# Seven block products for eight in the down projection of a decoder layer

## The chip, the cores and the metric

The kernel runs on one core of a Trainium2 chip. The metric is the time of the kernel on the device in microseconds (us), the median of several runs. A profile of one execution is read beside the times.

## The reference

One decoder layer on 256 tokens of width 2048: a token mixer, a cross-attention and a gated feed-forward block, each with a norm before and after. Only the last block matters here:

```python
def conv_glu_ffn(h, w_up, conv_w, conv_b, w_down):
    u = h @ w_up
    uc = conv_b + sum(conv_w[j] * shift_right(u, CONV_WIDTH - 1 - j) for j in range(CONV_WIDTH))
    gate, up = split_cols(uc, (D_FF, D_FF))
    return (jax.nn.gelu(gate, approximate=True) * up) @ w_down
...
x = x + rms_norm(conv_glu_ffn(h, ffn_w_up[l], ...), ffn_post_norm[l])
```

The down projection is the product with `w_down`: 256 x 8192 by 8192 x 2048, in float32.

## The kernel before

**Float32 by parts.** TensorE multiplies in a reduced float32 type (`F32R`). Each operand is split into a high part (a cast to that type, on ScalarE) and a low part (the operand less the cast, on VectorE). A product is then three matmuls: high by high, low by high, high by low (`tm_products`, L467). The weights' parts are `wh` (`Feed.hi`, L431) and `wl` (`Feed.lo`, L457). The down projection's activations are kept as `ac`, 64 tiles of 128 features by 256 tokens (`actile`, L1701), and are split into `as` just before use (`asplit`, L1788), two tiles to a buffer, with two buffers (`au0`, `au1`). `split` (L239) makes one ScalarE cast and one VectorE subtraction for each tile.

**The order of the work.** All engines run in the order in which the program issues their instructions. `run` (L475) goes through a list of blocks. A block is one group of output columns; for each chunk of weights it asks the feed for the staged weights of the chunk up to three ahead (`feed.lo(i + 3)`, L511), for transfers up to seven ahead (`feed.dma(i + 7)`, L512; four `raw` buffers, filled through the queue of SP), takes the activations (`b["xs"](k)`, L510) and issues the products (L545). Between products `side.half()` lets a piece of other work, such as the evacuation of the block before, into the ScalarE and VectorE queues.

**The down projection** is the last two blocks (L1915), one for each half (1024) of the output columns. A chunk is one k tile of 128 features: 128 x 1024 weights, 512 KB. Both halves go through all 64 k tiles. For each k tile there are four PSUM banks, two token tiles by two column groups of 512, and three matmuls of 128x128 by 128x512 into each: twelve to a tile. The first half's four banks come from the pool `aux`, the second's from `acc`; together the pools have the eight banks of PSUM. The last four tiles of the second half are done bank by bank (`tail`, L556), so that its evacuation (`fd_evac`, L1842) can follow each bank. `asplit` for the next pair of tiles is called at each even tile (`ax`, L1800), so ScalarE's cast waits until TensorE has left the buffer of two pairs before.

The stage before it is the up projection (`fm` blocks). It ends with the evacuation of its last block (`fw_evac`, L1747), which makes the last `ac` tile. Its inputs `fx` lie in the buffer `hT`, which the end of the kernel uses again: `load_gain` (L1833), called at tile 24 of the first half, takes it over for the gain of the last norm and for half of the output.

Of the kernel before, what the change touches and what calls it, by code (L numbers as in the profile page):

```python
# [9 lines left out]
F32 = mybir.dt.float32  # L10
# [5 lines left out]
P = 128  # L16
D = 2048
S = 256
# [136 lines left out]
def _layer(ctx, tc, nc, d, dbg):  # L155
# [22 lines left out]
    def C(name, tag, shape=None, dt=F32):  # L178
        return mp.tile(shape or [P, S], dt, tag=tag, bufs=1, name=name)
# [10 lines left out]
    def mm(out, lhsT, rhs, start=True, stop=True):  # L190
        pe.matmul(out, lhsT, rhs, start=start, stop=stop, skip_group_check=True)  # L191
# [47 lines left out]
    def split(hi, lo, src):  # L239
        act.copy(hi, src)  # L240
        dve.tensor_sub(lo, src, hi)
# [138 lines left out]
    blocks = []  # L380

    def block(kind, srcs, xs, evac, before=None, cols=512, pool_=None, pre=None, bankwise=False, tail=0,
              two=False, wide=None):


        blocks.append(dict(kind=kind, srcs=srcs, xs=xs, evac=evac, before=before, cols=cols,
                           pool=pool_ or acc, pre=pre, task=None, bankwise=bankwise, tail=tail, two=two, wide=wide is not None, xw=wide))
        return blocks[-1]

    class Feed:  # L390
        def __init__(self):
            a, g = blocks[0]["srcs"], blocks[1]["srcs"]
            self.src = a[:LEAD] + [c for p in zip(a[LEAD:], g) for c in p] + g[len(a) - LEAD:]
            self.src += [s for b in blocks[2:] for s in b["srcs"]]
            self.raw, self.st, self.nd, self.ns, self.nl, self.nop = {}, {}, 0, 0, 0, 0

        def dma(self, upto):
# [33 lines left out]
        def hi(self, upto):  # L431
            while self.ns <= min(upto, len(self.src) - 1):
                self.dma(self.ns)
                r = self.raw[self.ns]
                wh = self.staged("wh", r)
                for o, v in self.pieces(self.ns, wh, r):
                    nc.scalar.copy(o, v)  # L437
                self.st[self.ns] = [wh, None]
                self.ns += 1

        def first(self, c):

# [14 lines left out]
        def lo(self, upto):  # L457
            self.hi(upto)
            while self.nl <= min(upto, len(self.src) - 1):
                r = self.raw.pop(self.nl)  # L460
                wl = self.staged("wl", r)
                for o, v, h in self.pieces(self.nl, wl, r, self.st[self.nl][0]):
                    nc.vector.tensor_sub(o, v, h)  # L463
                self.st[self.nl][1] = wl
                self.nl += 1

    def tm_products(o, t, c, wx, first, last):  # L467
        wh, wl, xh, xl = wx
        t = slice(t // P * P, t // P * P + P)
        wh, wl = (turns(w[:, c:c + 512]) for w in (wh, wl))  # L470
        mm(o, xh[:, t], wh, start=first, stop=False)
        mm(o, xl[:, t], wh, start=False, stop=False)
        mm(o, xh[:, t], wl, start=False, stop=last)

    def run():  # L475
        feed = Feed()
# [6 lines left out]
        def work(b):  # L483
# [14 lines left out]
            nt = len(b["srcs"]) if b["bankwise"] else b["tail"]  # L498
            if nt:
                b["srcs"], tail = b["srcs"][:-nt], b["srcs"][-nt:]  # L500
            for ci, s in enumerate(b["srcs"]):
                second = b["two"] and ci % 2
                if second:
                    k -= s.shape[1]
                if b["pre"]:
                    b["pre"](ci, feed)
                feed.lo(i + 1)
                side.half(True)
                side.more = lambda: feed.hi(i + 2)
                ahead = b["xs"](k)  # L510
                feed.lo(i + 3)  # L511
                feed.dma(i + 7)  # L512
                wh, wl = feed.st.pop(i)
                later = []
                for kj in range(s.shape[1]):
                    xh, xl = b["xs"](k) if kj else ahead
                    first, last = k == 0, k == nk - 1
                    if b["wide"]:
                        xw = b["xw"](k).rearrange("p h (a b) -> p h b a", a=2)
                        for m in range(nm):  # L520
                            a, c = (w[:, kj, m * P:(m + 1) * P] for w in (wh, wl))
                            mm(banks[m].rearrange("p h s -> p (h s)"), a, xw, start=first, stop=False)
                            mm(banks[m][:, 0], c, turns(xh), start=False, stop=last)
                    elif b["kind"] == "fm":
                        xh, xl = turns(xh), turns(xl)
                        for m in range(nm):
                            r = min(P, b["cols"] - m * P)
                            o = banks[second * 2 + m // 2][0:r, m % 2]
                            a, c = (w[:, kj, m * P:m * P + r] for w in (wh, wl))
                            mm(o, a, xh, start=(first and m % 2 == 0), stop=False)  # L530
                            if not (b["two"] and ci == 0):
                                mm(o, a, xl, start=False, stop=False)
                            mm(o, c, xh, start=False, stop=last)
                        if b["two"] and ci == 0:
                            later.append((kj, xl))
                        for j, v in later if len(later) == s.shape[1] else ():
                            for m in range(nm):
                                mm(banks[m // 2][:, m % 2], wh[:, j, m * P:(m + 1) * P], v, start=False, stop=False)
                    elif b["cols"] < 512:
# [67 lines left out]
    def W(name, blk):  # L607
        return [d[name][blk, c] for c in range(d[name].shape[1])]
# [1177 lines left out]
    M["as"] = {}  # L1786

    def asplit(k):  # L1788

        if k not in M["as"]:  # L1790
            n = k // 2
            a = mp.tile([P, 1024], F32R, tag=f"au{n % 2}", bufs=1, name="as")
            a = a.rearrange("p (i j s) -> p i j s", i=2, j=2)
            a, b_ = a[:, 0], a[:, 1]
            for j in range(2):
                split(a[:, j], b_[:, j], actile((k + j) % 64))
                M["as"][k + j] = (a[:, j], b_[:, j])
        return M["as"][k]

    def ax(n):  # L1800
        def xs(k):
            kk = n * 64 + k
            if kk == 58:
                side.need(fu["task"])
            if kk == 24:
                load_gain()
            if k % 2 == 0:
                asplit(kk)
                if kk + 2 < 128 and (k < 62 or n == 0):
                    asplit(kk + 2)  # L1810
            return M["as"].pop(kk)
        return xs

    def x_tokens():

        M["xt"] = []
        for f in range(4):
# [9 lines left out]
            for b in range(4):  # L1827
                for c in range(4):
                    act.copy(o[b * 32:b * 32 + 32, :, :, c], q[c * 32:c * 32 + 32, :, :, b].rearrange("p k t i -> p t k i"))
                    if c % 2:  # L1830
                        yield

    def load_gain():  # L1833
        end = mp.tile([P, 2, 2, 1024], F32, tag="hT", bufs=1, name="end")
        M["gain"], M["z3", 1] = end[:, 0].rearrange("p t c -> p (t c)"), end[:, 1]
# [6 lines left out]
    def fd_evac(n):  # L1842
# [69 lines left out]
            yield  # L1912
        return gen

    for n in range(2):  # L1915
        block("tm", W("w_fd", n), ax(n), fd_evac(n), cols=1024, pool_=acc if n else aux,
              tail=4 if n else 0)
    run()
    drain_bulk()

# [100 lines left out]
```

## Time and profile before

| | before |
|---|---|
| median of 3 runs | 1804.07 us (1803.82 to 1804.76) |
| span of the profiled execution | 1802.7 us |
| its own time | only the span is given |
| TensorE (PE) busy | 1793.1 us |
| VectorE (DVE) busy | 1325.1 us |
| ScalarE (ACT) busy | 1056.8 us |
| down projection: 1463.46 us to the end of its matmuls | 331.54 us, 1536 matmuls |
| mean granted TensorE clock | 0.999 |

Times in the profile are in us from the span's start. A matmul's busy time is longer than its share of the stream, as matmuls overlap: in an unbroken stretch the length divided by the count is what one costs. In the rows, `tm` and `fm` are PSUM banks, `wh`, `wl`, `as`, `raw` the tiles named above, and `tm<-wh,as` is the product of the two into the bank. L191 is the helper that issues every matmul, L68 the one that issues most ScalarE and VectorE operations, so tiles tell more than lines. `x128 | 48.6, 422` reads: 128 instructions, 48.6 us in all, 422 ns each; behind the second bar stands the engine's idle time ahead of them and who ended it. A timeline's row gives the start, the length of a merged run of instructions, and in brackets the idle time before it.

### The profile page before, as it was taken

How to read it: one execution, taken by the hardware profiler on the slowest of the kernel's cores; microseconds unless marked ns; L12 is line 12 of the kernel's file. 1: busy time of each engine (PE TensorE's matmuls, PEld its weight loads, DVE VectorE, ACT ScalarE, POOL GpSimd, SP SyncE). 2: the span in 40 equal slices, each digit the busy share in tenths (PEclk: the TensorE clock that was granted, in tenths of full speed). 3: DMA queues.
4: the chain of work that ended last, by engine and by line, in shares of the span. 5: the costliest groups of instructions: out<-in, count | busy, mean ns of one | idle time of the engine just before them, and what ended most of it. 6: DMA issues, size and time to landing. Idle time of an engine off the chain costs nothing.

```text
span 1802.7 us, 30168 instructions
## 1 busy us (share of the span) xinstructions
PE 1793.1 (99%) x11814; PEld 1636.5 (91%) x11814; DVE 1325.1 (74%) x1948; ACT 1056.8 (59%) x1642; POOL 28.7 (2%) x51
## 2 busy tenths in 40 slices
PE   9999999999999999999999999999999999999998
PEld 8999988888888999899999999999999988888887
DVE  7869995765765768789877788777777775666665
ACT  7576454654554665676666666665565564455454
POOL 0100000100100000000000000000000000000000
PEclk9999999999999999999999999999999999999999
DMA  8656564354556775556666666666666666666664
GB/s 282 206 170 187 164 188 151 120 177 154 188 190 207 246 233 176 187 170 189 210 199 201 208 195 204 209 194 201 207 195 200 205 203 218 208 204 207 201 200 151
DMA packets 99135, 351.61 MB, mean 195 GB/s; under 512 B 10896, under 2 KB 13968, under 8 KB 98864
## 3 DMA queue, kind: packets, MB, share of 16 engines
q1 hardware_dynamic: 97888, 347.38, 60.4%
q8 instruction: 93, 1.52, 0.3%
q0 software_dynamic: 384, 1.18, 0.3%
q10 hardware_dynamic: 720, 1.12, 0.2%
q14 instruction: 50, 0.41, 0.1%
HBM read 347.01 MB, written 2.10 MB: 194 GB/s over the span
## 4 chain that ended last, share of the span: by engine, by line
PE 99%; DVE 0%; DMA 0%; ACT 0%; issue 0%; SPq 0%; DVEq 0%; ACTq 0%
PE fm L191 55%; PE tm L191 39%; PE gram L191 0%; PE Y L191 0%; PE lv L191 0%; DMA op<-in_op_dram 0%; PE X L191 0%; PE num L191 0%; PE zwa L191 0%; PE U L191 0%; PE gramA L191 0%; PE xo L191 0%; PE zg L191 0%; PE Tn L191 0%; PE mT L1353 0%; PE st L191 0%
## 5 line engine op out<-in xcount | busy, mean ns | idle before, releaser
L463 DVE TENSOR_TENSOR wl<-raw,wh 128x1024 fp32r<-128x1024 f32 (+1 forms) x641 | 767.9, 1219 | 145.8 <-ACT wh L437 143.4
L437 ACT CAST wh<-raw 128x1024 fp32r<-128x1024 f32 (+1 forms) x641 | 656.0, 1044 | 109.7 <-PE tm L191 60.7
L191 PE MATMUL fm<-fx,wh 128*128 128x512 f32 (+1 forms) x2240 | 672.8, 364 | 0.6 <-DVE fx L68 0.4
L191 PE MATMUL fm<-fx,wl 128*128 128x256 f32 x2048 | 558.3, 273 | 0.0
L191 PEld LDWEIGHTS fm<-fx,wh 128*128 128x128 f32 x2240 | 409.2, 190 | 49.8 <-DVE fx L68 1.0
L191 PEld LDWEIGHTS fm<-fx,wl 128*128 128x128 f32 x2048 | 393.2, 192 | 0.0
L191 PE MATMUL tm<-wh,as 128*128 128x512 f32 x1024 | 304.6, 379 | 0.0
L191 PE MATMUL tm<-wh,hx 128*128 128x512 f32 (+1 forms) x832 | 243.9, 378 | 1.8 <-ACT hx L68 1.5
L191 PEld LDWEIGHTS tm<-wh,as 128*128 128x128 f32 x1024 | 193.5, 189 | 27.4
L191 PE MATMUL tm<-wl,as 128*128 128x512 f32 x512 | 194.0, 379 | 0.0
L68 ACT COPY ul<-fm 128x256 f32<-128x256 f32 x128 | 44.9, 373 | 225.1 <-PE fm L191 225.1
L191 PE MATMUL fm<-hx,wh 128*128 128x256 f32 x1024 | 174.5, 277 | 0.0
L191 PEld LDWEIGHTS tm<-wh,hx 128*128 128x128 f32 x832 | 151.0, 189 | 22.5 <-POOL wh L450 1.7
L191 PEld LDWEIGHTS fm<-hx,wh 128*128 128x128 f32 x1024 | 155.4, 192 | 1.1
L191 PE MATMUL tm<-wl,hx 128*128 128x512 f32 (+1 forms) x416 | 152.5, 373 | 0.1
L68 DVE TENSOR_TENSOR us<-fm,ul 128x256 f32<-128x256 f32 x128 | 48.5, 421 | 130.9 <-ACT ul L68 130.9
L191 PE MATMUL fm<-hx,wl 128*128 128x256 f32 x512 | 140.8, 275 | 0.0
L68 ACT CAST as<-ac 128x256 fp32r<-128x256 f32 x128 | 45.6, 405 | 153.0 <-PE tm L191 153.0
L68 DVE TENSOR_TENSOR as<-ac,as 128x256 fp32r<-128x256 f32 x128 | 48.6, 422 | 91.3 <-ACT as L68 91.3
L191 PEld LDWEIGHTS tm<-wl,as 128*128 128x128 f32 x512 | 96.8, 189 | 13.7
L191 PEld LDWEIGHTS fm<-hx,wl 128*128 128x128 f32 x512 | 98.3, 192 | 0.0
L191 PEld LDWEIGHTS tm<-wl,hx 128*128 128x128 f32 x416 | 77.5, 189 | 10.7 <-DVE wl L463 0.3
(374 smaller groups left out, 1883.8 us busy)
## 6 DMA issues: line engine op xcount, KB each, us to landing
raw<-in_w_fw_dram SPq DMA_DIRECT2D x232, 512.0 KB, 4.2
raw<-in_w_in_dram SPq DMA_DIRECT2D x160, 512.0 KB, 3.7
raw<-in_w_fd_dram SPq DMA_DIRECT2D x128, 512.0 KB, 4.0
raw<-in_w_br_dram SPq DMA_DIRECT2D x32, 512.0 KB, 4.3
raw<-in_w_mw_dram SPq DMA_DIRECT2D x24, 512.0 KB, 4.6
raw<-in_w_fu_dram SPq DMA_DIRECT2D x24, 512.0 KB, 4.0
raw<-in_w_mo_dram SPq DMA_DIRECT2D x8, 512.0 KB, 4.2
raw<-in_w_xk_dram SPq DMA_DIRECT2D x8, 512.0 KB, 4.3
```

Source lines behind the costliest of these rows:

```text
L68: return f(out, *a, **k)
L191: pe.matmul(out, lhsT, rhs, start=start, stop=stop, skip_group_check=True)
L437: nc.scalar.copy(o, v)
L463: nc.vector.tensor_sub(o, v, h)
```

## The change

Two neighbouring k tiles with two token tiles and two column groups make a product of two 2 x 2 block matrices: eight block products of three matmuls each. For seven pairs of tiles of each half (tiles 6 and 7, 14 and 15, to 54 and 55) the change computes the same sums with seven block products (the Strassen-Winograd form). In one of the fourteen pairs:

- VectorE makes four sums of blocks of weights (`sums`): three when the first tile of the pair is staged, one of them in place of the raw block, and one when the second is. The first three need both tiles' raw weights. Two low parts of the sums are added to `lo`, two ScalarE casts (1024 and 512 wide) to `hi`.
- VectorE makes four sums of blocks of activations in three instructions and splits them (one cast, one subtraction, 512 wide), in `asplit`.
- TensorE does 7 x 3 matmuls. Three of the products go straight into three of the old banks; the other four into four more banks (`more`), taken from the other pool, which collect over the seven pairs.

After the last pair the extra banks are combined and added into the four old banks by VectorE (`join_sums`). The first steps are issued at tile 56, the four additions into the banks at tile 57, each right behind that tile's products into the bank. The buffer `hT` is taken over at the first sum (`room`), and the split of `ac` is done for two tiles by one cast and one subtraction of 512, in all 64 pairs of tiles.

```diff
@@ class Feed
         def hi(self, upto):
             while self.ns <= min(upto, len(self.src) - 1):
                 self.dma(self.ns)
+                if self.ns in self.pairs:
+                    self.sums(self.ns)
                 r = self.raw[self.ns]
                 wh = self.staged("wh", r)
...
+                if self.pairs.get(self.ns, (0, 0))[1]:
+                    M["ts"] = [C("ts", f"bg{j}", [P, 1024], F32R) for j in range(2)], [T2("t4", [P, 512], F32R) for _ in range(2)]
+                    nc.scalar.copy(M["ts"][0][0], M["sums"][:, 0:1024])
+                    nc.scalar.copy(M["ts"][1][0], M["sums"][:, 1024:])
                 self.ns += 1
+
+        def sums(self, c):
+            if self.pairs[c][1] == 0:
+                self.dma(c + 1)
+                if "sums" not in M:
+                    room()
+                b11, b12, b22 = self.raw[c][:, 0, 0:512], self.raw[c][:, 0, 512:], self.raw[c + 1][:, 0, 512:]
+                t = M["sums"]
+                nc.vector.tensor_add(t[:, 0:512], b22, b12)
+                nc.vector.tensor_sub(b12, b12, b11)
+                nc.vector.tensor_add(t[:, 512:1024], b22, b12)
+            else:
+                t = M["sums"]
+                nc.vector.tensor_sub(t[:, 1024:], self.raw[c][:, 0, 0:512], t[:, 512:1024])
...
@@ lo
+                if self.pairs.get(self.nl, (0, 0))[1]:
+                    t, (a, c) = M["sums"], M["ts"]
+                    nc.vector.tensor_sub(a[1], t[:, 0:1024], a[0])
+                    nc.vector.tensor_sub(c[1], t[:, 1024:], c[0])
...
+    def seven_products(b, banks, ci, w0h, w0l, w1h, w1l):
+        sv = b["seven"]
+        new = "more" not in sv
+        if new:
+            sv["ready"]()
+            sv["more"] = [sv["pool"]("more") for _ in range(4)]
+        (t, t4), a, sa = M["ts"], M["a4"].pop(0), M["sa"].pop(0)
...
+        old, more = banks, sv["more"]
+        for n, (o, x, w) in enumerate(((more[0], [v[:, 0] for v in a], half((w0h, w0l), 0)),
+                                       (old[0], [v[:, 2] for v in a], half((w1h, w1l), 0)),
+                                       (more[2], [v[:, 1] for v in sa], half((w0h, w0l), 1)),
+                                       (old[1], [v[:, 3] for v in sa], half((w1h, w1l), 1)),
+                                       (more[3], [v[:, 0] for v in sa], tops(0)),
+                                       (more[1], [v[:, 2] for v in sa], tops(1)),
+                                       (old[2], [v[:, 3] for v in a], t4))):
+            wh, wl = (turns(v) for v in w)
+            mm(o, x[0], wh, start=new and o in more, stop=False)
+            mm(o, x[1], wh, start=False, stop=False)
+            mm(o, x[0], wl, start=False, stop=ci == sv["at"][-1] and o in more)
...
+    def join_sums(banks, more):
+        u, v, p = (M["join"][:, i] for i in range(3))
+        act.copy(p, more[0])
+        dve.tensor_add(u, p, more[1])
+        dve.tensor_add(v, u, more[2])
+        yield
+        dve.tensor_add(banks[0], banks[0], p)
+        yield
+        dve.tensor_add(banks[1], banks[1], v)
+        dve.tensor_add(u, u, more[3])
+        yield
+        dve.tensor_add(banks[2], banks[2], u)
+        dve.tensor_add(v, v, more[3])
+        yield
+        dve.tensor_add(banks[3], banks[3], v)
+        yield
...
@@ work
-                feed.lo(i + 1)
+                pair = 1 if b["seven"] and ci in b["seven"]["at"] else 0
+                feed.lo(i + 1 + pair)
...
-                feed.lo(i + 3)
-                feed.dma(i + 7)
+                feed.lo(i + 3 + pair)
+                feed.dma(i + 7 + pair)
+                if join == 2:
+                    b["seven"]["joins"] = join_sums(banks, b["seven"]["more"])
+                    next(b["seven"]["joins"])
...
+                            if join == 3:
+                                next(b["seven"]["joins"])
...
+    SEVEN = [6 + 8 * i for i in range(7)]
...
             a = a.rearrange("p (i j s) -> p i j s", i=2, j=2)
-            a, b_ = a[:, 0], a[:, 1]
+            src = M["ac"][e // 16][:, e % 16:e % 16 + 2] if e < 32 else M["ac"][2 + (e - 32) // 8][:, e % 8:e % 8 + 2]
+            split(a[:, 0], a[:, 1], src)
             for j in range(2):
-                split(a[:, j], b_[:, j], actile((k + j) % 64))
-                M["as"][k + j] = (a[:, j], b_[:, j])
+                M["as"][k + j] = (a[:, 0, j], a[:, 1, j])
+            if e in SEVEN:
...
+                dve.tensor_sub(f[:, 0:2], x[:, 1:2].broadcast_to((P, 2, P)), x[:, 0:4:3])
+                dve.tensor_sub(f[:, 2], x[:, 0], f[:, 1])
+                dve.tensor_sub(f[:, 3], x[:, 2], f[:, 2])
+                sa = [T2("sa", [P, 4, P], F32R) for _ in range(2)]
+                split(sa[0], sa[1], f)
+                M["sa"].append(sa)
```

Here `join` is the tile's distance from 54, `old` the four banks of the half, `ready` the end of the evacuation that the extra banks wait for. In program order the first three sums come with tile p - 3 (by `feed.lo(i + 3)`), the sums of the activations with tile p - 2, the fourth sum and the low parts of the sums behind them.

More of the change, by code (lines that the diff above doesn't have):

```diff
@@ L382, in block @@
     def block(kind, srcs, xs, evac, before=None, cols=512, pool_=None, pre=None, bankwise=False, tail=0,
-              two=False, wide=None):
+              two=False, wide=None, seven=None):
         blocks.append(dict(kind=kind, srcs=srcs, xs=xs, evac=evac, before=before, cols=cols,
-                           pool=pool_ or acc, pre=pre, task=None, bankwise=bankwise, tail=tail, two=two, wide=wide is not None, xw=wide))
+                           pool=pool_ or acc, pre=pre, task=None, bankwise=bankwise, tail=tail, two=two, wide=wide is not None, xw=wide,
+                           seven=seven))
         return blocks[-1]
@@ L394, in __init__ @@
             self.src += [s for b in blocks[2:] for s in b["srcs"]]
+            n, self.pairs = sum(len(b["srcs"]) for b in blocks[:2]), {}
+            for b in blocks[2:]:
+                if b["seven"]:
+                    for k in b["seven"]["at"]:
+                        self.pairs[n + k], self.pairs[n + k + 1] = (b, 0), (b, 1)
+                n += len(b["srcs"])
             self.raw, self.st, self.nd, self.ns, self.nl, self.nop = {}, {}, 0, 0, 0, 0
@@ L473, in tm_products @@
         mm(o, xh[:, t], wl, start=False, stop=last)
+    def seven_products(b, banks, ci, w0h, w0l, w1h, w1l):
[5 more added lines that the diff above has]
+        (t, t4), a, sa = M["ts"], M["a4"].pop(0), M["sa"].pop(0)
+        half = lambda w, c: [v[:, 0, c * 512:c * 512 + 512] for v in w]
+        tops = lambda c: [v[:, c * 512:c * 512 + 512] for v in t]
+        old, more = banks, sv["more"]
[10 more added lines that the diff above has]
+            mm(o, x[0], wl, start=False, stop=ci == sv["at"][-1] and o in more)
+            if n in (1, 3, 5):
+                side.half()
+    def join_sums(banks, more):
[14 more added lines that the diff above has]
+        yield
     def run():
@@ L500, in work @@
                 b["srcs"], tail = b["srcs"][:-nt], b["srcs"][-nt:]
+            skip = False
             for ci, s in enumerate(b["srcs"]):
+                if skip:
+                    skip = False
+                    continue
+                join = b["seven"] and ci - b["seven"]["at"][-1]
                 second = b["two"] and ci % 2
@@ L510, in work @@
                 ahead = b["xs"](k)
-                feed.lo(i + 3)
-                feed.dma(i + 7)
+                feed.lo(i + 3 + pair)
[3 more added lines that the diff above has]
+                    next(b["seven"]["joins"])
                 wh, wl = feed.st.pop(i)
                 later = []
+                if b["seven"] and ci in b["seven"]["at"]:
+                    seven_products(b, banks, ci, wh, wl, *feed.st.pop(i + 1))
+                    k, i, skip = k + 2, i + 2, True
+                    yield
+                    continue
                 for kj in range(s.shape[1]):
@@ L1784, in _layer @@
         fu = block("fm", W("w_fw", f - 6), fu_xs(f), fw_evac(f), cols=256, wide=lambda k: M["fx"][:, :, k])
-    M["as"] = {}
+    M["as"], M["a4"], M["sa"] = {}, [], []
+    SEVEN = [6 + 8 * i for i in range(7)]
     def asplit(k):
         if k not in M["as"]:
-            n = k // 2
+            n, e = k // 2, k % 64
+            actile(e + 1)
             a = mp.tile([P, 1024], F32R, tag=f"au{n % 2}", bufs=1, name="as")
             a = a.rearrange("p (i j s) -> p i j s", i=2, j=2)
-            a, b_ = a[:, 0], a[:, 1]
+            src = M["ac"][e // 16][:, e % 16:e % 16 + 2] if e < 32 else M["ac"][2 + (e - 32) // 8][:, e % 8:e % 8 + 2]
+            split(a[:, 0], a[:, 1], src)
             for j in range(2):
-                split(a[:, j], b_[:, j], actile((k + j) % 64))
-                M["as"][k + j] = (a[:, j], b_[:, j])
+                M["as"][k + j] = (a[:, 0, j], a[:, 1, j])
+            if e in SEVEN:
+                four = lambda v: v.rearrange("p k (t s) -> p (k t) s", t=2)
+                M["a4"].append([four(a[:, i]) for i in range(2)])
+                if "f4" not in M:
+                    room()
+                x, f = four(src), M["f4"]
+                dve.tensor_sub(f[:, 0:2], x[:, 1:2].broadcast_to((P, 2, P)), x[:, 0:4:3])
[4 more added lines that the diff above has]
+                M["sa"].append(sa)
         return M["as"][k]
@@ L1831, in x_tokens, with room @@
                         yield
+    def room():
+        end = mp.tile([P, 2 * KD * S], F32, tag="hT", bufs=1, name="end")
+        M["gain"], M["z3", 1] = end[:, 0:2048], end[:, 2048:4096].rearrange("p (t c) -> p t c", t=2)
+        M["sums"], M["f4"] = end[:, 4096:5632], end[:, 5632:6144].rearrange("p (k s) -> p k s", k=4)
+        M["join"] = end[:, 6144:7680].rearrange("p (i c) -> p i c", i=3)
     def load_gain():
-        end = mp.tile([P, 2, 2, 1024], F32, tag="hT", bufs=1, name="end")
-        M["gain"], M["z3", 1] = end[:, 0].rearrange("p t c -> p (t c)"), end[:, 1]
         sp.dma_start(M["gain"], d["fpg"].partition_broadcast(P))
@@ L1913, in fd_evac, with fd_ready @@
         return gen
+    def fd_ready(n):
+        return lambda: side.need(fd[0]["task"] if n else fu["task"])
+    fd = []
     for n in range(2):
-        block("tm", W("w_fd", n), ax(n), fd_evac(n), cols=1024, pool_=acc if n else aux,
-              tail=4 if n else 0)
+        fd.append(block("tm", W("w_fd", n), ax(n), fd_evac(n), cols=1024, pool_=acc if n else aux,
+                        tail=4 if n else 0, seven=dict(at=SEVEN, pool=aux if n else acc, ready=fd_ready(n))))
     run()
```

## The prediction

> **What bounds the kernel now.** I read the page first, then the chain of waits in order of time, then the last stage alone.
>
> ```profile
> span 1802.7 us, 30168 instructions
> ...
> PE 1793.1 (99%) x11814; PEld 1636.5 (91%) x11814; DVE 1325.1 (74%) x1948; ACT 1056.8 (59%) x1642; POOL 28.7 (2%) x51
> ...
> PE 99%; DVE 0%; DMA 0%; ACT 0%; issue 0%; SPq 0%; DVEq 0%; ACTq 0%
> ```
>
> TensorE is busy in all of the span, and 99% of the chain that ends last is TensorE. The next question is what the changed stage, the down projection, looks like in that chain and in a window of half of it (its length, then the busy time of PE, PEld, DVE, ACT and POOL, the granted clock, the DMA share, GB/s).
>
> ```profile
> 1463.46 331.54 PE tm L191 x1536
> ...
> 1463.46:1629.20 165.74, 165.74 (x769) 145.13 (x769) 102.97 (x135) 86.78 (x134) 0.00 (x0) 1.00 0.65 210
> ```
>
> The down projection is one unbroken piece of the chain: 1536 matmuls in 331.54 us, 215.85 ns each, at a granted clock of 1.00. A k tile has 12 of them, so it takes 2.59 us, and a pair of tiles 5.18 us. In this stage VectorE is busy 102.97 of 165.74 us (62%). How the two staging engines follow TensorE is seen in two stretches of their timelines:
>
> ```profile
> L191 PE MATMUL tm<-wh,as x1024: 379/379/382, 1463.3 to 1794.4; 128*128 128x512 f32 x171
> ...
> 1499.76 0.71 ACT L68 CAST as<-ac 128x256 fp32r<-128x256 f32 x2 [2.57 <-PE tm L191]
> 1500.38 1.99 ACT L437 CAST wh<-raw 128x1024 fp32r<-128x1024 f32 x2
> 1504.94 0.71 ACT L68 CAST as<-ac 128x256 fp32r<-128x256 f32 x2 [2.57 <-PE tm L191]
> ...
> 1500.20 0.76 DVE L68 TENSOR_TENSOR as<-ac,as 128x256 fp32r<-128x256 f32 x2 [1.56 <-ACT as L68]
> 1501.45 2.36 DVE L463 TENSOR_TENSOR wl<-raw,wh 128x1024 fp32r<-128x1024 f32 x2 [0.50 <-ACT wh L437]
> 1505.38 0.76 DVE L68 TENSOR_TENSOR as<-ac,as 128x256 fp32r<-128x256 f32 x2 [1.56 <-ACT as L68]
> ```
>
> The first matmul of the stage starts at 1463.3, so tile 14 starts at 1463.3 + 14 x 2.59 = 1499.56, and ScalarE's split of the activations (`as`) starts 0.20 later, released by TensorE: the two `as` buffers tie ScalarE, and VectorE behind it, to TensorE once per pair. Each period then holds two `as`, two `wh`, two `wl`, and VectorE rests 1.56 + 0.50 us of 5.18. So TensorE is the bound, with about 2 us of slack on VectorE per pair. That slack is what the change spends.
>
> **The change, part by part.** *Products.* A pair needs 7 x 3 = 21 matmuls instead of 24, all of the same shape. Fourteen pairs drop 42 matmuls: 42 x 0.21585 = 9.07 us off the path, and a pair takes 4.53 us instead of 5.18.
>
> The Trainium skill ("TensorE: Matmul & The Clock Gate", Back-to-back issue gap) gives about 131 ns for such a matmul in a real kernel's stream; by it the drop would be 42 x 0.131 = 5.5 us and the sum below 3.6 us worse. The 215.85 ns of this trace decides against it.
>
> *Work added on VectorE and ScalarE.* I need the durations, and the distance from one start to the next where nothing is waited for:
>
> ```profile
> L463 DVE TENSOR_TENSOR wl<-raw,wh 128x1024 fp32r<-128x1024 f32 x149 | 176.4, 1221 | 29.8 <-ACT wh L437 29.8
> L437 ACT CAST wh<-raw 128x1024 fp32r<-128x1024 f32 x149 | 149.7, 1044 | 0.4
> L68 DVE TENSOR_TENSOR as<-ac,as 128x256 fp32r<-128x256 f32 x128 | 48.6, 422 | 91.3 <-ACT as L68 91.3
> L68 ACT CAST as<-ac 128x256 fp32r<-128x256 f32 x128 | 45.6, 405 | 153.0 <-PE tm L191 153.0
> L68 DVE TENSOR_TENSOR us<-us,stf_b 128x512 f32<-128x512 f32 x7 | 4.8, 693 | 0.2
> L68 DVE TENSOR_TENSOR end<-tm,end 128x512 f32<-128x512 f32 x4 | 2.8, 689 | 2.6 <-ACT jk L68 2.6
> ...
> 1453.09 0.76 DVE L68 TENSOR_TENSOR us<-fm,ul 128x256 f32<-128x256 f32 x2 [2.29 <-ACT ul L68]
> 1453.88 0.69 DVE L68 TENSOR_TENSOR us<-us,stf_b 128x512 f32<-128x512 f32 x1
> 1454.49 1.22 DVE L463 TENSOR_TENSOR wl<-raw,wh 128x1024 fp32r<-128x1024 f32 x1
> ```
>
> A VectorE addition takes 1.22 (1024 wide), 0.69 (512, from PSUM as from SBUF) or 0.42 (256); 128 wide, by the step from 512 to 256, 0.29. The next one starts after 1.14 (2.36 for two, less 1.22), 0.61 (1453.88 to 1454.49) and 0.34; one that needs the result waits for the end (1453.88 is 0.03 after two of 0.76). ScalarE takes 1.04 or 0.405, so 0.62 for 512 wide; its starts are 0.95, 0.52 and 0.31 apart. A hand-over between engines is 0.04.
>
> Per pair VectorE gets four sums of weights (4 x 0.61 and one wait), the low parts of the sums (1.14 + 0.61), three sums of activations (1.07 with their waits) and their low part (0.61): 6.0 us. The split two tiles at once gives back 0.07 per pair of tiles. In eight tiles VectorE had 8 x 1.14 + 8 x 0.34 = 11.8 us of work; it gets 17.5 of 20.07 us. It fits on average. But the additions come in a heap, so I follow one pair of tiles p, p+1, with time 0 where TensorE starts tile p-2, and TensorE due at p at 5.18.
>
> The split for p-2 is released 0.2 after -5.18, at -4.97 (unrounded). ScalarE: `as` 0.62, then `wh`(p-1) from -4.45 to -3.41; VectorE: `wl`(p-1) at -3.37, then at -2.23 the three sums of weights, of which the second holds `wh`(p) (ScalarE, -0.90 to 0.14); `wl`(p) at 0.18. The split of p, p+1 is released at 0.2; its low part on VectorE comes behind `wl`(p), at 1.32; the sums of activations run from 1.92 to 3.00, ScalarE's cast of them to 3.66, their low part at 3.70. Then the fourth sum at 4.30, `wl`(p+1) from 4.90 to 6.12, the low parts of the sums to 7.26 and 7.87, `wl`(p+2) to 9.00, `as`(p+2) to 9.61. TensorE needs `wl`(p+1) for its sixth matmul of the pair, at 5.18 + 5 x 0.216 = 6.26, the sums' low parts at 8.20 and 9.49, and `as`(p+2) at 9.71 + 0.22 = 9.93. So everything is just in time: the margins are 0.1 us at `wl`(p+1) and 0.3 at `as`(p+2). VectorE is 1.5 to 2 us behind afterwards and catches up in the tiles between two pairs.
>
> Its first sum also needs the weights of p+1 landed. Their transfer is issued behind `wl`(p-3):
>
> ```profile
> raw<-in_w_fd_dram SPq DMA_DIRECT2D x121, 512.0 KB, 4.0
> end<-in_fpg_dram SPq DMA_DIRECT2D x1, 1024.0 KB, 7.5
> ...
> DMA to landing us min/median/max: 3.4/4.0/5.9
> ```
>
> Where the pair before has pushed that `wl` to its late place (13.6 after that pair's zero, so -6.4 here), it lands at -2.4, 0.2 before the sum at -2.23; the slowest of the stretch, 5.9, would be 1.7 late. Late transfers push the whole heap, but a stall of TensorE also moves its next due times back, so about half of a lateness stays. Between nothing and 12 x 0.8 = 10 us for the twelve pairs that follow another, I take 0.1 each, 1.2 us, near the median's end. The 1 MB gain load (7.5 us) stands in the queue just ahead of the weights of one pair: 0 to 1.7, I take 0.3. The split of the last two tiles, on the path at the end, is one wide cast instead of two: 0.1.
>
> *The join.* This is the term that decides. Behind the last pair (tiles 54, 55 of each half) VectorE adds three combinations into the four banks that TensorE is still accumulating in. Bank 0 is added after its product of tile 57, and tile 58 must wait for the addition; so must banks 1 to 3. ScalarE's copy of the first extra bank costs nothing, as ScalarE has rested. In the time of the last pair, VectorE's queue after the sums' low parts (next start 7.78) is: `wl`(56), `as`(56), `wl`(57), `wl`(58), `as`(58), `wl`(59), two join sums (0.73 with the wait, 0.60), `wl`(60), the addition to bank 0: 5 x 1.14 + 2 x 0.61 + 1.33 + 0.69, which ends at 16.7. TensorE is due at bank 0 of tile 58 at 9.71 + 2 x 2.59 = 14.89: it stalls 1.9. Bank 1 is ready in time. Before bank 2 and before bank 3 stands one more addition whose result is needed, so they are ready 1.9 (18.63) and 3.3 (19.96) after bank 0, while TensorE reaches them 0.65 apart: 0.6 and 0.7 more. That is 3.2 us a half, 6.4 in all. Bounds: had VectorE no backlog at all, bank 0's addition could end at 13.85 (TensorE's product at 12.95, 0.21 for the release, 0.69) and bank 3's at 17.1, against 16.83 due: 0.3 a half. If every wait inside the heap vanished (0.34 + 0.48 + 0.70 us before `wl`(p-1), `wl`(p) and the cast), 1.7. Nothing in the rows makes VectorE's queue shorter than that, so I take 3.2. That TensorE is kept from a bank while VectorE is in it is a rule of the program, not a price in time: the Trainium skill ("PSUM — Partial Sum Buffer", PSUM bank collisions raise a hardware error) says that two engines in one bank at once is an error and must be kept apart by a wait; no run here shows it.
>
> *The rest.* Two waits for banks are new:
>
> ```profile
> 1463.57 0.76 DVE L68 TENSOR_TENSOR us<-fm,ul 128x256 f32<-128x256 f32 x2 [0.94 <-ACT ul L68]
> ...
> 1634.43 0.68 DVE L68 TENSOR_TENSOR z<-tm,end 128x512 f32<-128x512 f32 x1
> ```
>
> The extra banks of the first half need the last feed-forward block's evacuation, whose additions start at 1463.57, fifteen us ahead of tile 6 (1463.3 + 6 x 2.59 = 1478.8). Those of the second half need the first half's evacuation, whose last product ends at 1635.1, before tile 6 of that half (1463.3 + 70 x 2.59 = 1644.6). The tile that held the inputs of the up projection is taken over earlier, but TensorE has left it by 1463.3. Nothing, for each; the cover is nine us or more.
>
> **Sum:** -9.07 + 6.4 + 1.2 + 0.3 + 0.1 = -1.1 us on the profiled execution, 1802.7 to 1801.6. The median of the runs lies 1.4 above that span (1804.07), so 1803.0.
>
> **The rivals.** *A: the join is hidden.* If VectorE is earlier in its queue than I have it, each 0.1 us is worth 0.2. From 1.25 us earlier the total passes -3.6. With the heap's waits gone the joins cost 3.3 and the time is 1804.07 - 9.07 + 3.3 + 0.4 to 1.6 = 1798.7 to 1800; wholly hidden, 0.6 and 1796 to 1797. For it: VectorE's average load leaves 2.5 us in eight tiles. Against it: these rests lie elsewhere, and nine instructions are queued in front of bank 0.
>
> *B: the pairs stall.* The place is the sixth matmul of a pair, which waits for `wl`(p+1); margin 0.1. If the heap is later by 0.6 us (a transfer of 4.6 instead of 4.0 and the sums' waits a little longer), 0.5 stays in each of fourteen pairs, 7 us, and the total is 1804.07 - 9.07 + 6.4 + 7 + 0.4 = 1808.8. It decides from 0.42 us of stall a pair (5.9 us in all, +3.6). For it: no slack is left in my schedule, and the transfers come closer together after a pair. Against it: half of a lateness heals, and the median transfer fits.
> The Trainium skill ("VectorE: DVE Perf Modes", The DRAIN you can't avoid) would bring this about by itself: the next VectorE operation does not start until the pipe has emptied. Then six operations ahead of `wl`(p+1) would each cost 0.08 more, and the joins about 0.9 more each: near 1809. The rows show starts 1.14 apart for operations of 1.22, so of B's 0.15 it has 0.01.
>
> **How the numbers follow.** Forecast 0.55, A 0.30, B 0.15. 0.2% is 3.6 us, about what a measurement of this kernel can tell from no change; the forecast's own range, 1800.5 to 1806.5, lies inside it, A is faster, B slower: faster 0.30, same 0.55, slower 0.15. The range takes in half to two thirds of A and the beginning of B: 1797.5 to 1807.3.
>
> **What would show it.** Right: TensorE's count falls from 11814 to 11772; the chain of waits shows two breaks, at tile 58 of either half, about 3 us each, released by VectorE's additions into `tm`; elsewhere the pairs take 4.53 us with gaps of a few tenths at most; VectorE's busy time in the stage rises by some 90 us; the stage is 330 us long. Wrong: gaps inside each pair before the matmuls with `wl` (B), or none at tile 58 and a stage of 323 us (A). If the stage shortens by 9 us and the span does not, I have mislaid the end.

## The result and the profile after

The changed kernel takes 1817.12 us (1814.33 to 1817.52), against 1804.07 before, each the median of five runs: the ratio is 1.0068, with a 95% interval of 1.0057 to 1.0079. That is 13 us slower where 1 us faster was forecast, and above the range. The profiled execution has a span of 1815.6 us, 12.9 above that of before. Its page:

```profile
span 1815.6 us, 30152 instructions
...
PE 1792.6 (99%) x11772; PEld 1628.3 (90%) x11772; DVE 1409.1 (78%) x2040; ACT 1080.7 (60%) x1622; POOL 28.6 (2%) x51
```

The 42 matmuls are gone (11772 instead of 11814), and yet TensorE's busy time is all but unchanged, at 99%. That number hides the loss, because a matmul counts as busy to its modelled end. What is lost shows in the waits of the down projection (who waits for whom: total us, times, longest us):

```profile
ACT wh L446 <- DVE raw L463: 40.9, 12, 6.4
...
PEld tm L191 <- DVE wl L491: 10.7, 14, 1.2
...
DVE end L462 <- DMA raw<-in_w_fd_dram: 7.7, 9, 3.6
PE tm L191 <- ACT wh L446: 6.0, 5, 1.9
...
PE tm L191 <- DVE wl L491: 5.1, 8, 0.8
...
PE tm L191 <- DVE tm L68: 1.7, 4, 0.5
...
raw<-in_w_fd_dram SPq DMA_DIRECT2D x122, 512.0 KB, 4.3
```

Before, no TensorE matmul of the stage waited. Now it waits for weights (`wl`, `wh`) and for the join (`DVE tm`, and, as shown below, 3.5 of the 6.0 us put down to `wh`); VectorE's first sum of a pair (L462) waits nine times for its weights' transfer, and the median transfer takes 4.3 us instead of 4.0.

I added up, over the starts of all matmuls of the stage, what lies between them beyond 215.85 ns each. The two joins: 3.35 us each. The first pair of either half: 0.1 and 0.2. The fourth pair of the first half: 5.5. The other eleven pairs: 9.1 in all, from 0.15 to 1.8. The last tiles: 0.2. Together 21.7; less the 9.07 saved, that makes 12.7 of the 12.9 us.

**The join** is as the prediction has it. VectorE, then TensorE, around tile 58 of the first half:

```profile
1619.26 1.22 DVE L491 TENSOR_TENSOR wl<-raw,wh 128x1024 fp32r<-128x1024 f32 x1
1620.40 1.29 DVE L68 TENSOR_TENSOR tm<-tm,end 128x512 f32<-128x512 f32 x2
1621.60 0.68 DVE L68 TENSOR_TENSOR end<-end,more 128x512 f32<-128x512 f32 x1
1622.38 0.70 DVE L68 TENSOR_TENSOR tm<-tm,end 128x512 f32<-128x512 f32 x1
1622.98 0.68 DVE L68 TENSOR_TENSOR end<-end,more 128x512 f32<-128x512 f32 x1
1623.77 0.70 DVE L68 TENSOR_TENSOR tm<-tm,end 128x512 f32<-128x512 f32 x1
...
1619.12 0.38 PE L191 MATMUL tm<-wl,as 128*128 128x512 f32 x1
1621.23 0.67 PE L191 MATMUL tm<-wh,as 128*128 128x512 f32 x2 [1.74 <-ACT wh L446]
...
1623.13 0.70 PE L191 MATMUL tm<-wh,as 128*128 128x512 f32 x2 [0.36 <-DVE tm L68]
...
1624.52 0.70 PE L191 MATMUL tm<-wh,as 128*128 128x512 f32 x2 [0.48 <-DVE tm L68]
```

TensorE is due at 1619.34 and starts tile 58 at 1621.23, right after VectorE's first addition into a bank (1620.40 + 0.70); the row names ScalarE's `wh`, but that is the cast for a later tile, which happened to end at the same time. Two more waits of 0.5 and 0.6 follow the additions into banks 2 and 3, and behind each of the three waits the next matmul is another 0.1 late.

**A pair that follows another** loses time in a ring. This is the chain of waits from one pair's weights to the next (start, length, what; "issue" is time for which the profile shows no wait):

```profile
1662.35 4.98 DMA raw<-in_w_fd_dram
...
1667.42 0.70 DVE end L462
...
1668.92 1.05 ACT wh L446
...
1669.99 1.23 DVE wl L491
1671.22 0.60 DVE as L68
...
1672.85 0.63 ACT sa L68
...
1674.79 1.14 DVE wl L491
...
1683.44 4.34 DMA raw<-in_w_fd_dram
...
1674.64 0.59 PE L191 MATMUL tm<-wh,as 128*128 128x512 f32 x2
1675.98 0.48 PE L191 MATMUL tm<-wl,as 128*128 128x512 f32 x1 [0.75 <-DVE wl L491]
```

The transfer takes 4.98 us, the sums start when it has landed, and then VectorE, but for two hand-overs to ScalarE (the casts `wh` and `sa`), works on through the sums, the split, the sums of the activations and everything after, until the buffer is free for the next pair's transfer at 1683.44. Round the ring it is 21.1 us, and TensorE needs 20.07 for the eight tiles. TensorE is not in the ring: it waits 0.9 us for `wl` at the sixth matmul (1674.64 + 0.43 = 1675.07 due, 1675.98 started), and its waiting does not shorten the ring.

The other pairs agree. The flight of the second tile's weights, from issue to landing in the trace, is 4.11 to 5.74 us for the eleven pairs, 4.6 in the median, and each pair loses what its flight has above 4.0 us, to within 0.05 us: 4.98 and 1.0 lost here, 4.34 and 0.4 for the next, 5.74 and 1.8 for the longest.

**The gain load** makes one pair worse. VectorE's first sum, then TensorE, then two windows (length, busy of PE, PEld, DVE, ACT, POOL; then the granted clock):

```profile
1528.42 1.22 DVE L491 TENSOR_TENSOR wl<-raw,wh 128x1024 fp32r<-128x1024 f32 x1
...
1537.88 0.69 DVE L462 TENSOR_TENSOR end<-raw 128x512 f32<-128x512 f32 x1 [3.62 <-DMA raw<-in_w_fd_dram]
...
1542.34 0.48 PE L191 MATMUL more<-wh,as 128*128 128x512 f32 x1 [0.65 <-DVE as L68]
...
1544.92 0.70 PE L191 MATMUL tm<-wh,as 128*128 128x512 f32 x2 [1.89 <-ACT wh L446]
1546.44 0.79 PE L191 MATMUL tm<-wl,as 128*128 128x512 f32 x1 [0.82 <-DVE wl L491]
1547.03 1.06 PE L191 MATMUL more<-wh,sa 128*128 128x512 f32 x2
1547.88 0.63 PE L191 MATMUL more<-wl,sa 128*128 128x512 f32 x1
...
1543.50:1547.00 3.50, 1.26 (x3) 0.80 (x4) 3.04 (x4) 3.50 (x5) 0.00 (x0) 0.84 0.28 112
1547.00:1551.00 4.00, 4.00 (x15) 3.30 (x14) 4.00 (x6) 2.71 (x4) 0.00 (x0) 0.72 0.65 163
```

The weights of the pair's second tile are asked for at 1529.66, when `wl` has freed their buffer (1528.42 + 1.22) and right behind the gain load. They land at 1537.86, 8.2 us later, and VectorE stands 3.62 us. TensorE then waits three times, 0.65, 1.89 and 0.82 us, and for some matmuls behind that runs at half clock (two in 0.85 us, from 1547.03 to 1547.88). The flight is 4.2 us above 4.0, and the half clock costs another 1.4: together the 5.5 us of this pair.

### The profile page after: what moved, and what is told of

It reads as the page before. It is cut to its first block, busy times and chain, and to the rows that moved or that the text cites. A ratio compares the mean times of both kernels' runs of the same rounds, so it can differ in the third digit from the quotient of the medians.

```text
span 1815.6 us, 30152 instructions
## 1 busy us (share of the span) xinstructions
PE 1792.6 (99%) x11772; PEld 1628.3 (90%) x11772; DVE 1409.1 (78%) x2040; ACT 1080.7 (60%) x1622; POOL 28.6 (2%) x51
## 5 line engine op out<-in xcount | busy, mean ns | idle before, releaser
L191 PE MATMUL tm<-wh,as 128*128 128x512 f32 x828 | 247.4, 380 | 7.8 <-ACT wh L446 6.0
L191 PEld LDWEIGHTS tm<-wh,as 128*128 128x128 f32 x828 | 155.6, 189 | 33.7 <-ACT wh L446 8.5
L191 PE MATMUL tm<-wl,as 128*128 128x512 f32 x414 | 158.7, 383 | 5.5 <-DVE wl L491 5.1
L191 PEld LDWEIGHTS tm<-wl,as 128*128 128x128 f32 x414 | 78.3, 189 | 21.4 <-DVE wl L491 10.7
L191 PE MATMUL fm<-mg,wh 128*128 128x512 f32 (+1 forms) x320 | 84.9, 340 | 0.0
L191 PE MATMUL fm<-mg,wl 128*128 128x256 f32 x256 | 69.9, 273 | 0.0
```

## The experiments

Theory: the pairs are late because the row of work on VectorE and the transfer make a ring with no reserve. Rivals: a pair is too much work for VectorE wherever it stands; or the wide split delays the staging. All times are beside runs of the kernel before on the same chip, 1804.4 to 1804.5.

**The wide split alone.** The kernel before, with only this part:

```diff
-                split(a[:, j], b_[:, j], actile((k + j) % 64))
+            split(a[:, 0], a[:, 1], src)
```

> The kernel before with one part of the change alone: activations split two tiles at once, no block products. Expected is no difference but the 0.1 us at the last two tiles, which lie on the path: 1804.4 to 1804.6 where the kernel before takes 1804.4. A difference over 1 us would mean that the wide split is what delays the staging.

Measured: 1804.37 us, ratio 1.0000 (0.9991 to 1.0008). This part costs and gives nothing that can be measured.

**Four pairs a half, 16 tiles apart.**

```diff
-    SEVEN = [6 + 8 * i for i in range(7)]
+    SEVEN = [6 + 16 * i for i in range(4)]
```

> Four pairs a half, 16 tiles apart (6, 22, 38, 54), instead of seven, 8 apart; the join is as it was. The products saved are 8 x 3 x 0.216 = 5.2 us, the joins cost 6.5. Theory one (a pair is only late where the pair before it has pushed back the weights' transfers): each pair loses about 0.1, in all 2 to 2.5 us more than before: 1806 to 1807. Theory two (each pair overflows by itself, by the 0.8 us that the eleven lose on average): 8 x 0.8 us more: about 1812.

Measured: 1807.08 us, ratio 1.0015 (1.0006 to 1.0023), as theory one has it. In the waits of its stage, TensorE waits for no `wl`, and no sum waits for a transfer; the joins are left (the first row is their wait at tile 58, put down to `wh` as above):

```profile
PE tm L191 <- ACT wh L446: 3.5, 2, 1.7
...
PE tm L191 <- DVE tm L68: 1.7, 4, 0.5
```

Each of the eight pairs loses 0.1 to 0.2 us. A pair on its own does fit. In the six that follow another pair, the second tile's weights fly 3.4 to 3.5 us.

**The gain load late.**

```diff
-            if kk == 24:
+            if kk == 58:
```

> The load of the last norm's gain is issued at tile 58 of the first half instead of tile 24; nothing else changes. Theory one (the pairs stall where the weights of the second tile of a pair land late, and the 1 MB gain load in front of the weights of the fourth pair is the worst case): the 5.5 us that the fourth pair of the first half loses in the changed kernel's trace shrink to the 0.1 to 1.5 of the others, so 4 to 5.4 us less than the changed kernel: about 1812.5 us where the kernel before takes 1804. Theory two (VectorE has too much to do in a pair, whenever the transfers land): the fourth pair loses much the same, at most 1 us is won: 1816 to 1817.

Measured: 1812.38 us, ratio 1.0041 (1.0029 to 1.0053), 4.7 us less than the changed kernel. The fourth pair now loses 0.5 us, and the granted clock stays at 1.00 through the stage. The other eleven still lose, 8.8 us in all:

```profile
DVE end L462 <- DMA raw<-in_w_fd_dram: 6.3, 11, 1.3
PE tm L191 <- DVE wl L491: 5.5, 11, 0.8
```

Again each of the twelve pairs that follow another loses what its flight (4.24 to 5.57 us) has above 4.0 us, to within 0.05.

**Half of the second tile's weights.** On top of the late gain load, the second tile of each pair gets only half of its weights, so the result lacks the rest:

```diff
+                    if self.pairs.get(self.nd, (0, 0))[1]:
+                        sp.dma_start(r[:, :, 512:], s[:, :, 512:])
+                        pool.memset(r[:, :, 0:512], 0.0)
+                    else:
+                        sp.dma_start(r, s)
```

> The changed kernel with the gain load at tile 58, and for the second tile of each pair only half of the weights are loaded (256 KB; GpSimd writes zeros in the other half), which leaves out part of the product. The row of work on VectorE and its place are the same; the transfer that the first sum waits for lands earlier by some 0.7 to 1 us. With the gain load late alone the time is 8 us above the kernel before. Theory one (a late transfer starts the row of work late): the pairs lose 0.1 to 0.3 each instead of 0.8, so about 6 us less: about 1806. Theory two (the row of work is too long in itself, whenever it starts): within 1 us of the kernel with the late gain load, 1811.5 to 1812.5.

Measured: 1805.59 us, ratio 1.0006 (0.9997 to 1.0015), 6.8 us less than with the late gain load alone. VectorE has the same work; only the transfer is shorter (3.5 to 4.5 us in the twelve pairs). Its waits:

```profile
PE tm L191 <- DVE wl L495: 0.7, 2, 0.5
...
DVE end L466 <- DMA raw<-in_w_fd_dram: 0.2, 1, 0.2
```

The first sum waits once for 0.2 us instead of 6.3 us in all, and TensorE waits twice for `wl` instead of eleven times. So it is the landing of the transfer that makes the row late, and theory two falls.

**The sums of the activations early.** Same work, another place:

```diff
     def asplit(k):
...
-                x, f = four(src), M["f4"]
...
-                M["sa"].append(sa)
         return M["as"][k]
+
+    def act_sums(e):
+
+        if e in SEVEN:
...
+            x, f = four(src), M["f4"]
...
+            M["sa"].append(sa)
...
         def xs(k):
...
+            act_sums(k + 5)
             if k % 2 == 0:
                 asplit(kk)
```

> The sums of a pair's activations and their split are issued five tiles ahead of the pair instead of two. This takes some 2.4 us out of the row of work between the low part of the first tile's weights and that of the second; the amount of work stays. Theory one (the row of work has no reserve, so a transfer that lands 1 us late is passed on to TensorE): the eleven pairs that lose 9 us in all lose about 1, the pair behind the gain load 3 instead of 5.5: 10 us less than the changed kernel, about 1807. Theory two (VectorE's work as a whole is too much for eight tiles): nothing or up to 2 us is won, 1815 to 1817.

Measured: 1800.91 us, ratio 0.9981 (0.9972 to 0.9989): 16 us less than the changed kernel, 6 more than I expected. No pair waits, not even the one behind the gain load. Waits, and VectorE ahead of one pair:

```profile
PE tm L191 <- DVE tm L68: 3.6, 6, 0.9
...
DVE end L462 <- DMA raw<-in_w_fd_dram: 1.7, 1, 1.7
...
1650.58 0.41 DVE L68 TENSOR_TENSOR end<-ac 128x256 f32<-128x256 f32 x1
1651.03 0.62 DVE L68 TENSOR_TENSOR end<-ac,end 128x128 f32<-128x128 f32 x2
1652.34 0.69 DVE L68 TENSOR_TENSOR sa<-end,sa 128x512 fp32r<-128x512 f32 x1 [0.69 <-ACT sa L68]
...
1656.16 0.69 DVE L462 TENSOR_TENSOR end<-raw 128x512 f32<-128x512 f32 x1
...
1661.08 1.22 DVE L491 TENSOR_TENSOR wl<-raw,wh 128x1024 fp32r<-128x1024 f32 x1
```

The sums of the activations (1650.58 to 1653.0) now run while the weights are in flight, where VectorE had stood waiting. Only one sum waits for a transfer, 1.7 us, behind the gain load, and the reserve takes it up. The joins also fall, to 2.6 us each, because VectorE is less far behind. My expectation missed this: a shorter row also frees the buffers earlier, so the transfers are not late any more.

**The join late.** All sums first, and the additions two tiles later:

```diff
...
         dve.tensor_add(u, u, more[3])
+        dve.tensor_add(w, v, more[3])
+        yield
+        for bank, part in zip(banks, (p, v, u, w)):
+            dve.tensor_add(bank, bank, part)
+            yield
...
-                            if join == 3:
+                            if join == 5:
```

> All four sums of the join are made at tile 56 and the four additions into the banks are issued at tile 59 instead of 57, with nothing between them. Theory (VectorE reaches the additions 1.9 us after TensorE is due at the bank, and the sums between the additions cost the rest): the join's 3.3 us a half become about 0.8, so 5 us less than the changed kernel: about 1812. Rival (the wait only moves to another tile, since VectorE stays as far behind): under 1 us less, 1816 to 1817.

Measured: 1813.15 us, ratio 1.0054 (1.0042 to 1.0066), 4 us less than the changed kernel. Either join now costs 0.9 to 1.0 us, but in the second half 1.8 come back in the last four tiles, where TensorE waits for the split of the activations that stands behind the additions. Both sides were right, for one half each. The joins give only 3.0 of the 4 us; in the profiled execution the rest is that the fourth pair loses 3.5 us instead of 5.5, mainly as the granted clock did not fall there, while the other pairs lose some 1 us more. The six runs go from 1811.35 to 1817.7 us, so the 4 us are not firm.

**The three together**, the second half's additions one tile earlier (`add` is 5 in the first half and 4 in the second):

```diff
-                            if join == 3:
+                            if b["seven"] and join == b["seven"]["add"]:
```

> The three edits together: gain load at tile 58, sums of the activations five tiles ahead, all four sums of the join at tile 56 with the four additions at tile 59 in the first half and 58 in the second, ahead of its last four tiles. With the sums early alone the time was 3.5 us under the kernel before, and its trace has only the joins left, 2.4 us a half. Theory: the join of the first half falls to some 0.2 and that of the second to about 1.4, so 3 us less: about 1797.5 where the kernel before takes 1804. Rival (what the join gives up comes back as late activations in the last tiles, as 1.8 us did with the late join alone): 1 to 2 us less, about 1799.

Measured: 1798.08 us, ratio 0.9964 (0.9952 to 0.9977). The first half's join costs 0.2 us; the second half keeps 1.6 at the join and 0.5 in its last tiles.

**Six pairs in the second half**, so that its join lies earlier:

```diff
+    AT = [SEVEN, SEVEN[:-1]]
...
-                        tail=4 if n else 0, seven=dict(at=SEVEN, pool=aux if n else acc, ready=fd_ready(n), add=4 if n else 5)))
+                        tail=4 if n else 0, seven=dict(at=AT[n], pool=aux if n else acc, ready=fd_ready(n), add=5)))
```

> The three edits together, with seven pairs in the first half and six in the second, whose join then lies at tiles 48 to 51, far from the last four tiles. The pair given up costs 0.65 us. With seven pairs the join and the last tiles of the second half kept TensorE waiting for 1.6 + 0.5 us. If the joins cost little wherever VectorE has rest, about 1.3 us less than with seven pairs in both halves: about 1796.8. If they cost as much at tile 51, 0.6 us more: 1798.7.

Measured: 1796.53 us, ratio 0.9956 (0.9944 to 0.9969), the fastest of all, 8 us under the kernel before. In its trace no pair waits, and either join costs 0.2 us: 39 matmuls saved are 8.4 us, and its profile's span is 8.3 under that of before (1794.4). Two stretches of its chain:

```profile
1724.10 16.19 PE tm L191 x75
1744.17 42.49 PE tm L191 x195
```

**Eight pairs**, with distances of 6 and 8 tiles in turn:

```diff
-    SEVEN = [6 + 8 * i for i in range(7)]
+    SEVEN = [6, 12, 20, 26, 34, 40, 48, 54]
...
+            act_sums(k + 6 if k in SEVEN else k + 5 if k - 1 not in SEVEN else 0)
```

> The three edits together with eight pairs a half instead of seven, the distances between pairs 6 and 8 tiles in turn. Two more pairs save 6 matmuls, 1.3 us. In 14 tiles with two pairs VectorE has about 32.2 us of work where TensorE needs 35.0. If that fits, 1.3 us less than with seven pairs, about 1796. If VectorE's rests can't be used at that distance, the second pair of each two stalls by 0.5 to 1 us, and the time is 1 to 3 us above that with seven pairs.

Measured: 1812.64 us, ratio 1.0044 (1.0031 to 1.0058), 14.6 us above seven pairs, worse than either side had it. I had put the sums of the close pairs ahead of the split that TensorE needs next, and that is what TensorE waits for. So once more, with those sums called behind the split, `asplit(kk + 2)`:

```diff
+            if k - 1 not in SEVEN and k + 5 not in (12, 26, 40, 54):
+                act_sums(k + 5)
...
+            if k + 4 in (12, 26, 40, 54):
+                act_sums(k + 4)
```

> Eight pairs a half again, but where two pairs are 6 tiles apart the sums of the second pair's activations are issued four tiles ahead of it and behind the split of the activations, not ahead of the split that TensorE needs next. In the first run with eight pairs TensorE's waits at the second pairs were for that split (ScalarE's cast of it stood behind the cast of the sums). If the place was the cause, the waits go and the time is 1.3 us below that with seven pairs: about 1797. If VectorE's work is too much at that distance, the waits come back as waits for the weights' low parts: 1800 or more.

Measured: 1804.77 us, ratio 1.0003 (0.9994 to 1.0012). The waits of the two (first the one with 1812.64 us):

```profile
PE tm L191 <- ACT as L68: 5.2, 8, 1.4
...
PE tm L191 <- DVE wl L491: 2.2, 4, 0.6
PE tm L191 <- DVE tm L68: 2.2, 1, 2.2
...
PE more L191 <- DVE as L68: 0.8, 3, 0.5
```

The place was 8 us of it. Of the 10.6 us that TensorE still loses, 6.5 lie in the second pairs of each two, as waits for `wl` and for the split's low part, both VectorE's work: at a distance of 6 tiles it comes late, though 32.2 us of work in 35.0 would fit on average. That the heaps are closer together than its rests is my reading of it; no run varies that alone. Another 3.9 us lie at the joins and in the last tiles (2.3 with seven pairs), where TensorE waits mostly for the addition into a bank.

## Why the prediction was wrong

*The saving* was right. 9.07 us are off the path: in the kernel with early sums, 75 matmuls take 16.19 us where nothing waits, 0.216 each. The other price weighed in the prediction, 131 ns, is refuted.

*The join* was right in place and size: 6.4 forecast, 6.7 measured, in the steps 1.9, 0.6, 0.7 that came out as 2.0, 0.6, 0.7, the late matmul behind each wait counted with it. That it need not be paid is shown by the version with six pairs in the second half.

*The schedule of one pair* was right. In the first pair of the first half `wl` of the second tile starts at 1478.88, 5.0 us after TensorE's start of the tile two before, where I had 4.90, and the sixth matmul starts on time.

*The step that failed* is "I take 0.1 each, 1.2 us, near the median's end" for the twelve pairs that follow another, and with it "about half of a lateness stays". Measured are 9.1 us for eleven of them, near the outer bound of 10 us that I had given all twelve and set aside, and 5.5 for the one behind the gain load, where I had 0.3 and a bound of 1.7: its weights flew 8.2 us, more than the slowest flight, 5.9, of the kernel before. Two things were wrong in it. I took the flight time from the kernel before, 4.0 us, though my own schedule asks for four transfers in some 4.6 us behind each pair; in the changed kernel the second tile's weights, the third of the four, take 4.6 in the median of the eleven pairs (4.3 is the median of all transfers of the stage). And I let TensorE's stall heal the lateness. It can't: the next transfer waits for VectorE, VectorE for the transfer, and TensorE is not in that ring. With 4.0 us of flight the ring is 20.1 us long, just what TensorE needs, so flight above that is lost in full, not by half: in 23 pairs of two kernels the loss is the flight less 4.0 us, to within 0.05. The experiment with half loads shows the flight as the cause, and the one with early sums shows the ring: 2.4 us taken out of it, and all of the pairs' loss is gone.

*Rival B* named the place (the sixth matmul, waiting for `wl`) and a transfer 0.6 late as the condition. It was the case that came, with a price of 7 us for what cost 14.9 in the fourteen pairs: it had the gain load at 0.3 instead of 5.5, and its own lateness still partly healed. Its chance of 0.15 was too low: a margin of 0.1 us, against a flight time whose own rows went from 3.4 to 5.9, is no margin. That VectorE's operations would not overlap was no part of it: in the rows of the join the next one starts 1.14 after one of 1.22 (1619.26 to 1620.40).

## What to carry to other kernels

Where a change puts work on an engine that hands buffers back to the transfers, draw the ring: landing, work, release, next landing. If it is as long as the stage's own period it has no reserve, and the bounding engine's waits do not heal it. Work that needs no new data belongs in the time in which the ring waits for its transfer; here moving 2.4 us of it made a loss of 13 us a gain of 3.5, and with the gain load late and the joins where the engine has rest, at the price of one pair, 8.

## What the runs showed of the hardware

Behind the gain load the granted clock fell to half for 3.4 us: 0.84 over 3.5 us and 0.72 over 4.0 us in the two windows are 1.1 and 2.2 us at half. It fell at about 1545.9, behind waits of 0.65 and 1.89 us and 0.2 us into the third, of 0.82, with matmuls between them. The first kernel with eight pairs had such a stretch behind waits of 1.31 and 0.33 us; the joins of the changed kernel, with 1.7, 0.4 and 0.5, had none, and neither had the 1.88 and 0.82 in the profiled execution of the kernel with the late join. So a stall can cost 1.4 us on top of its own length, and what decides is not the length of the waits alone; that stays open. The Trainium skill ("TensorE: Matmul & The Clock Gate", What's actually happening) has half rate after an idle window of about 3.4 us; the trace agrees in the half, and the stretch at half is as long as that window, but TensorE was not idle for so long before it.

A transfer of 512 KB took 4.0 us in the median of the kernel before, and 4.1 to 5.7 as the third of four asked for within about 4.3 us (1659.48 to 1663.74 at the pair shown); behind one of 1 MB in the same queue it took 8.2 us. With four pairs a half, where the transfers do not come so close together, the pair's weights took 3.4 to 3.5. No run separates the crowding from other causes of the longer flight.
